# One 512-column matmul moves both activation halves in the feed-forward of layers 1 to 3

## The chip, the cores and the metric

The kernel runs on one core of a Trainium2 chip. The metric is device time in microseconds (us): the median of three runs. TensorE (PE in the profile) multiplies, VectorE (DVE) and ScalarE (ACT) work element by element, GpSimd (POOL) and SyncE (SP) mainly issue transfers.

## The reference

Four layers over 256 tokens of width 1024; each layer has a token mixer (forgetting attention, a state-space layer, a pooling mixer, forgetting attention again) and then a dense SwiGLU. Everything is float32.

```python
def swiglu(h, w_gate_up, w_down):
    g, u = jnp.split(h @ w_gate_up, 2, axis=-1)
    return (jax.nn.silu(g) * u) @ w_down

for i in range(DEPTH):                       # DEPTH = 4, D_MODEL = 1024, D_FF = 2816
    x = x + mixer_i(rms_norm(x, mix_norm_g[i]))
    x = x + swiglu(rms_norm(x, ffn_norm_g[i]), ffn_w_gate_up[i], ffn_w_down[i])
return rms_norm(x, final_norm_g)
```

## The kernel before, in words

Activations are kept transposed: 8 blocks of 128 features, 256 tokens (N) in the free dimension. Near-float32 precision comes from splitting every matmul operand into a high and a low half in the fp32r format: a weight unit arrives by DMA as `raw` (128 x 1024), ACT casts it to the high half (line 98), and DVE subtracts to make the low half (line 99); both halves stand in one tile `hl`. The activations `X` and the hidden layer `H` have halves too. `term` (line 158) multiplies one 128 x 128 weight piece with one activation block in three matmuls of 256 columns: weight-high by X-high, weight-low by X-high, weight-high by X-low. They add up in the same 256 columns of a PSUM bank. Each of the three loads its own weights.

The feed-forward of a layer (`ffn`, line 239) has a gate-up part and a down part. Gate-up makes 22 pairs of a gate tile G and an up tile U; each of the 44 tiles is one weight unit and 8 terms (24 matmuls). The first four tiles (two pairs) are computed block by block of X, alternating between four banks; after that the tiles go one after the other through the four `P` banks, so the G of one pair takes the bank that the G two pairs earlier left. `act` evicts a pair: `t` = G times the row scale R on DVE (line 248), silu on ACT (line 249), `h` = U times t on DVE (line 251), and the split of `h` into H-high (ACT, line 178) and H-low (DVE, line 179). Down makes 8 blocks of 22 terms into two `acc` banks, scales each by R (line 273), adds it to the residual x (line 237) and prepares what the next layer needs (`settled`, line 181).

Each engine runs its instructions in the order in which they stand in its queue; that order comes from a scheduler that rearranges the program's own order. Weights are fetched through 4 `raw` buffers and cast into 5 `hl` buffers, so a cast waits until PE is done with the unit that stood five places earlier. `rstd` (line 210) forms R between the stages: a matmul with ones over the squares (`sq`), a power on POOL, two transposes on PE and a copy on ACT.

Of the kernel before, what the change touches and what calls it, by code (L numbers as in the profile page):

```python
# [9 lines left out]
F32 = mybir.dt.float32  # L10
F32R = mybir.dt.float32r
AF = mybir.ActivationFunctionType
ALU = mybir.AluOpType
# [4 lines left out]
N = 256  # L18
DFF = 2816
NCH = DFF // 128  # L20
# [13 lines left out]
class Trunk:  # L34
# [128 lines left out]
    def dense(self, outs, X, ready=None):  # L163
        hls = [self.unit() for _ in outs]
        for k in range(8):
            for out, hl in zip(outs, hls):
                self.term(out, hl, slice(128 * k, 128 * k + 128), X, k, k == 0, k == 7)
                if k % 2 or len(outs) > 1 and (out is outs[1] or out is outs[-1]):
                    self.tick()

    def new_X(self, pool=None):
        return (pool or self.ap).tile([128, 2, 8, N], F32R, tag="X", name="X", bufs=1)

    def work(self, name="wk"):
        return self.ap.tile([128, N], F32, tag="wk", name=name, bufs=6)

    def split(self, hi, lo, src):
        self.nc.scalar.copy(hi, src)  # L178
# [2 lines left out]
    def settled(self, d, key):  # L181

        nc, x = self.nc, self.x[:, d]
        if d == 0:
            self.sq = self.ap.tile([128, N], F32, tag="sq", name="sq", bufs=2)
            if key is not None and key != 2:
                self.X = self.new_X()
        if key is not None and key != 2:
            g = self.gT[:, 8 * key + d:8 * key + d + 1]
            nc.scalar.activation(self.X[:, 0, d], x, AF.Identity, scale=g)  # L190
            nc.vector.scalar_tensor_tensor(out=self.X[:, 1, d], in0=x, scalar=g, in1=self.X[:, 0, d].bitcast(F32),
                                           op0=ALU.mult, op1=ALU.subtract)
        if key == 2:
            self.at(2, lambda: self.to_tokens(d))
        if d == 0:
            nc.scalar.activation(self.sq, x, AF.Square, scale=1.0 / 32.0)
        else:
            s = self.work("s")
            nc.scalar.activation(s, x, AF.Square, scale=1.0 / 32.0)  # L199
            nc.vector.tensor_tensor(out=self.sq, in0=self.sq, in1=s, op=ALU.add)  # L200
        if key is None:
            if d == 0:
                self.xg = self.ap.tile([128, 8, N], F32, tag="X", name="xg", bufs=1)
# [35 lines left out]
    def ffn(self, l):  # L239
        nc = self.nc  # L240
        X, key = self.X, l + 1 if l + 1 < self.layers else None
        with self.tc.tile_pool(name="hidden", bufs=1, reuse_waits="tile") as hp:
            H = hp.tile([128, 2, NCH, N], F32R, name="H")
            R = self.R

            def act(i, G, U):
                t = self.work("t")
                nc.vector.tensor_tensor(out=t, in0=G, in1=R, op=ALU.mult)  # L248
                nc.scalar.activation(t, t, AF.Silu)  # L249
                h = self.work("h")  # L250
# [3 lines left out]
            outs = [self.bank(t)[:, 0:N] for t in ("acc", "acc", "P", "P")]  # L254
            self.dense(outs, X)
            act(0, outs[0], outs[1])
            act(1, outs[2], outs[3])
            for i in range(2, NCH):
                G, U = self.bank("P")[:, 0:N], self.bank("P")[:, 0:N]
                self.dense([G], X)  # L260
                self.dense([U], X)
                act(i, G, U)
            for d in range(8):
                o = self.bank("acc")[:, 0:N]
                for u, ks in enumerate((8, 8, 6)):
                    hl = self.unit()
                    for k in range(ks):
                        f = 8 * u + k
                        self.term(o, hl, slice(128 * k, 128 * k + 128), H, f, f == 0, f == NCH - 1)
                        if k % 2:  # L270
                            self.tick()
                t = self.work("t")
                nc.vector.tensor_tensor(out=t, in0=o, in1=R, op=ALU.mult)
                self.add(d, t)
                self.settled(d, key)

    def fox(self, l, j):
        nc, a, X = self.nc, self.a, self.X
# [5 lines left out]
        cols = (slice(0, 352), slice(352, 704), slice(704, 1040))  # L284
        seg = [[banks[3 * t + s][:, 0:cols[s].stop - cols[s].start] for s in range(3)] for t in range(2)]
        for k in range(8):
            hl = self.unit()
            for t in range(2):
                tok = slice(t * 128, t * 128 + 128)
                for s, (xs, ws) in enumerate(((0, 0), (0, 1), (1, 0))):  # L290
                    for o, c in zip(seg[t], cols):
                        self.mm(o, X[:, xs, k, tok], hl[:, ws, c], k == 0 and s == 0, k == 7 and s == 2)
                self.tick()
        rs, R = self.rs, self.R
        self.lf, self.nd, self.c = [], [], []
# [80 lines left out]
    def heads(self, hp, q, kT, oT):  # L376
# [40 lines left out]
        self.split(oT[:, 0, hp], oT[:, 1, hp], op[:, 0:N])  # L417

    def to_tokens(self, d):
        nc = self.nc  # L420
# [14 lines left out]
    def poolmix(self, l):  # L435
# [7 lines left out]
        for d in range(8):  # L443
            o = self.bank("acc")[:, 0:N]
            f = slice(d * 128, d * 128 + 128)
            self.mm(o[:, 0:128], self.xt[:, 0, f], sb0[:, d // 2, 0:128], True, False)
            self.mm(o[:, 128:256], self.xt[:, 1, f], sb1[:, d // 2], False, False)
            self.mm(o[:, 128:144], self.xt[:, 0, f], sb0[:, d // 2, 128:144], False, True)
            g = self.gT[:, 8 * l + d:8 * l + d + 1]
            nc.scalar.activation(X[:, 0, d], o, AF.Identity, scale=g)  # L450
            nc.vector.scalar_tensor_tensor(out=X[:, 1, d], in0=o, scalar=g, in1=X[:, 0, d].bitcast(F32),
                                           op0=ALU.mult, op1=ALU.subtract)
        for u in range(2):
            hl = self.unit()
# [379 lines left out]
    def emit(self, m, u, CX, KT, sx, G):  # L834
# [11 lines left out]
        self.split(G[:, 0, m], G[:, 1, m], g)  # L846
        self.emitted = m + 1

    def final(self):
# [128 lines left out]
```

## Time and profile before

| | |
|---|---|
| runs | 1190.84, 1191.64, 1192.45 us; median 1191.64 |
| the profiled execution | 1194.52 us; its span, first to last instruction, 1192.7 us |
| mean granted TensorE clock | 0.98 |
| PE busy | 1145.8 us, 96% of the span |
| DVE busy | 823.4 us, 69% |
| ACT busy | 622.3 us, 52% |

A busy PE is one with at least one matmul in its pipeline; a matmul's own row lasts longer than the distance to the next one, since neighbours overlap. The distance from start to start is therefore what a matmul costs in a dense row of them, and it is read from the first start of a merged row, its count, and the start of what follows.

### The profile page before, as it was taken

Reading aid. Unit: us, or ns where it says so; the run is one execution under the profiler, and the core shown is the slowest. Engines: PE = TensorE matmul, PEld = TensorE weight load, DVE = VectorE, ACT = ScalarE, POOL = GpSimd, SP = SyncE. Lnnn points to the kernel's source line nnn. Section 1 sums busy time; section 2 is a strip of 40 time slices with the busy share of each in tenths; the row PEclk is TensorE's granted clock in tenths of the full one; section 3 lists DMA queues with packets and bytes.
Section 4 is the critical chain, followed back from the end, with each engine's and each line's share of the span. In section 5 each row is a group of like instructions: output and inputs, shape, how many; then the busy total and the mean of one; then the engine's idle time right before and its main releaser. Section 6 shows DMA issues by size and latency. Waiting matters only on the chain. (4 is left out here: it accounts for less than half of the span.)

```text
span 1192.7 us, 25313 instructions
## 1 busy us (share of the span) xinstructions
PE 1145.8 (96%) x10238; PEld 1115.4 (94%) x10238; DVE 823.4 (69%) x1525; ACT 622.3 (52%) x1094; POOL 160.6 (13%) x186
## 2 busy tenths in 40 slices
PE   6989999999999999999999899999998999999996
PEld 6878999999999889999999899999997899999996
DVE  6799987877659766666655576665656677666563
ACT  5546777677743144544444564444445566544441
POOL 1288001111102210000000000000006730000000
PEclk9889999999999899999999899999999999999998
DMA  7645466777879626566566355666665554765561
GB/s 270 183 158 152 156 211 234 248 241 223 284 254 334 240 75 194 190 182 186 177 179 186 104 175 180 188 176 182 191 189 184 151 160 120 221 190 179 177 185 44
DMA packets 63492, 225.16 MB, mean 189 GB/s; under 512 B 7824, under 2 KB 8192, under 8 KB 63248
## 3 DMA queue, kind: packets, MB, share of 16 engines
q1 hardware_dynamic: 56304, 200.83, 54.5%
q0 software_dynamic: 6208, 21.64, 5.7%
q8 instruction: 80, 1.31, 0.4%
q10 hardware_dynamic: 864, 1.09, 0.3%
q14 instruction: 36, 0.29, 0.1%
HBM read 208.81 MB, written 14.71 MB: 187 GB/s over the span
## 5 line engine op out<-in xcount | busy, mean ns | idle before, releaser
L156 PE MATMUL P<-X,hl 128*128 128x256 f32 x5520 | 685.5, 284 | 0.0
L156 PEld LDWEIGHTS P<-X,hl 128*128 128x128 f32 x5520 | 668.3, 190 | 8.0 <-issue 7.5
L99 DVE TENSOR_TENSOR hl<-raw,hl 128x1024 fp32r<-128x1024 f32 (+3 forms) x363 | 438.3, 1208 | 209.0 <-ACT hl L98 205.7
L98 ACT CAST hl<-raw 128x1024 fp32r<-128x1024 f32 (+3 forms) x363 | 371.8, 1026 | 389.8 <-issue 174.9
L156 PE MATMUL acc<-H,hl 128*128 128x256 f32 x2112 | 253.6, 281 | 0.7 <-DVE H L179 0.7
L156 PEld LDWEIGHTS acc<-H,hl 128*128 128x128 f32 x2112 | 250.6, 188 | 1.5 <-DVE H L179 0.9
L156 PE MATMUL acc<-X,hl 128*128 128x256 f32 x480 | 71.1, 292 | 5.4 <-DVE X L179 3.6
L221 POOL TENSOR_TENSOR rs<-rs,mhalf 128x2 f32<-128x2 f32 x9 | 6.5, 724 | 486.4 <-DVE rs L220 486.4
L156 PEld LDWEIGHTS acc<-X,hl 128*128 128x128 f32 x480 | 62.4, 193 | 8.4 <-DVE X L179 4.4
L372 POOL TENSOR_SCALAR nb<-nb,c 128x128 f32<-128x128 f32 (+1 forms) x64 | 64.1, 1015 | 1.1
L251 DVE TENSOR_TENSOR h<-P,t 128x256 f32<-128x256 f32 x84 | 35.5, 422 | 30.6 <-PE P L156 30.6
L393 ACT ACTIVATE pt<-pt,st 128x128 f32<-128x128 f32 (+1 forms) x64 | 28.5, 446 | 30.0 <-DVE st L391 30.0
L248 DVE TENSOR_TENSOR t<-P,R 128x256 f32<-128x256 f32 x84 | 35.5, 422 | 10.6 <-PE P L156 8.0
L249 ACT ACTIVATE t<-t 128x256 f32<-128x256 f32 x88 | 36.5, 414 | 11.9 <-DVE t L248 11.7
L178 ACT CAST H<-h 128x256 fp32r<-128x256 f32 x88 | 35.3, 402 | 12.3 <-DVE h L251 12.3
L156 PE MATMUL P<-hl,X 128*128 128x336 f32 (+1 forms) x192 | 40.0, 330 | 0.0
L179 DVE TENSOR_TENSOR H<-h,H 128x256 fp32r<-128x256 f32 x88 | 36.9, 419 | 0.2 <-ACT H L178 0.2
L156 PE MATMUL acc<-hl,X 128*128 128x352 f32 x96 | 25.0, 343 | 10.2 <-ACT X L190 6.6
L190 ACT ACTIVATE X<-x,gT 128x256 fp32r<-128x256 f32 x56 | 28.3, 505 | 11.8 <-DVE x L237 7.6
L156 PEld LDWEIGHTS P<-hl,X 128*128 128x128 f32 x192 | 33.4, 197 | 0.0
L199 ACT ACTIVATE s<-x 128x256 f32<-128x256 f32 x63 | 25.6, 406 | 12.4 <-DVE x L237 12.4
L406 PE MATMUL tp<-cst,pt 128*128 128x128 f32 x96 | 18.2, 302 | 11.8 <-DVE pt L397 10.5
(165 smaller groups left out, 800.7 us busy)
## 6 DMA issues: line engine op xcount, KB each, us to landing
raw<-in_w_gu SPq DMA_DIRECT2D x176, 512.0 KB, 3.9
raw<-in_w_dn SPq DMA_DIRECT2D x64, 512.0 KB, 3.6
raw<-in_w_qk SPq DMA_DIRECT2D x32, 512.0 KB, 3.7
raw<-in_w_dn SPq DMA_DIRECT2D x32, 384.0 KB, 3.4
raw<-in_w_fo SPq DMA_DIRECT2D x16, 512.0 KB, 3.7
raw<-in_w_glu SPq DMA_DIRECT2D x16, 512.0 KB, 4.8
raw<-in_w_vf SPq DMA_DIRECT2D x15, 520.0 KB, 3.7
nb<-nd POOLq DMA_DIRECT2D x24, 256.0 KB, 5.8
```

The lines of the kernel that those rows point to most:

```text
L98: nc.scalar.copy(hl[:, 0, s], raw[:, s])
L99: nc.vector.tensor_tensor(out=hl[:, 1, s], in0=raw[:, s], in1=hl[:, 0, s].bitcast(F32), op=ALU.subtract)
L156: self.nc.tensor.matmul(out, lhsT=lhsT, rhs=rhs, start=start, stop=stop)
L178: self.nc.scalar.copy(hi, src)
L179: self.nc.vector.tensor_tensor(out=lo, in0=src, in1=hi.bitcast(F32), op=ALU.subtract)
L190: nc.scalar.activation(self.X[:, 0, d], x, AF.Identity, scale=g)
L199: nc.scalar.activation(s, x, AF.Square, scale=1.0 / 32.0)
L248: nc.vector.tensor_tensor(out=t, in0=G, in1=R, op=ALU.mult)
L249: nc.scalar.activation(t, t, AF.Silu)
L251: nc.vector.tensor_tensor(out=h, in0=U, in1=t, op=ALU.mult)
L372: nc.gpsimd.tensor_scalar(out=nb[:, i], in0=nb[:, i], scalar1=self.c[t][:, 4 * n + i:4 * n + i + 1], scalar2=None, op0=ALU.add)
L393: nc.scalar.activation(pt, pt, AF.Exp, bias=st[:, 0:1], scale=-1.0, accum_out=st[:, 1:2])
```

## The change

In the feed-forward of layers 1, 2 and 3 a term is two matmuls in place of three. The two halves of an activation block now lie next to each other (`[128, 8, 2, N]` in place of `[128, 2, 8, N]`, and the same for H), so that the high half of the weights moves both halves as 512 columns into a whole bank: columns 0 to 255 get weight-high by X-high, columns 256 to 511 get weight-high by X-low. The low half of the weights then moves X-high into columns 256 to 511. `fold` adds the two sums when the bank is evicted: ACT copies the second half of the bank to SBUF (`lo`), DVE adds it to the first half, and what was read from the bank before (the multiplication by R, or U times t) now reads that sum. Layer 0 and all mixers keep the three matmuls; only the indices of X and H change there. The work tiles have 8 buffers in place of 6, and `xg` has memory of its own.

```diff
     def term(self, out, hl, cols, X, k, start, stop):
-        self.mm(out, hl[:, 0, cols], X[:, 0, k], start, False)
-        self.mm(out, hl[:, 1, cols], X[:, 0, k], False, False)
-        self.mm(out, hl[:, 0, cols], X[:, 1, k], False, stop)
+        self.mm(out, hl[:, 0, cols], X[:, k, 0], start, False)
+        self.mm(out, hl[:, 1, cols], X[:, k, 0], False, False)
+        self.mm(out, hl[:, 0, cols], X[:, k, 1], False, stop)
...
+    def wide(self, o, hl, s, X, k, first, last):
+        self.mm(o, hl[:, 0, s], X[:, k].rearrange("p a n -> p (a n)"), first, False)
+        self.mm(o[:, N:], hl[:, 1, s], X[:, k, 0], False, last)
+
+    def fold(self, o):
+        nc = self.nc
+        lo, t = self.work("lo"), self.work("t")
+        nc.scalar.copy(lo, o[:, N:])
+        nc.vector.tensor_tensor(out=t, in0=o[:, 0:N], in1=lo, op=ALU.add)
+        return t
...
-            H = hp.tile([128, 2, NCH, N], F32R, name="H")
+            H = hp.tile([128, NCH, 2, N], F32R, name="H")
...
+            wide = l > 0
+            cut = (lambda z: z) if wide else (lambda z: z[:, 0:N])
...
             def act(i, G, U):
-                t = self.work("t")
-                nc.vector.tensor_tensor(out=t, in0=G, in1=R, op=ALU.mult)
+                t = self.fold(G) if wide else self.work("t")
+                nc.vector.tensor_tensor(out=t, in0=t if wide else G, in1=R, op=ALU.mult)
                 nc.scalar.activation(t, t, AF.Silu)
-                h = self.work("h")
-                nc.vector.tensor_tensor(out=h, in0=U, in1=t, op=ALU.mult)
-                self.split(H[:, 0, i], H[:, 1, i], h)
+                h = self.fold(U) if wide else self.work("h")
+                nc.vector.tensor_tensor(out=h, in0=h if wide else U, in1=t, op=ALU.mult)
+                self.split(H[:, i, 0], H[:, i, 1], h)
...
-                o = self.bank("acc")[:, 0:N]
+                o = cut(self.bank("acc"))
...
-                        self.term(o, hl, slice(128 * k, 128 * k + 128), H, f, f == 0, f == NCH - 1)
+                        s = slice(128 * k, 128 * k + 128)
+                        (self.wide if wide else self.narrow)(o, hl, s, H, f, f == 0, f == NCH - 1)
...
-                t = self.work("t")
-                nc.vector.tensor_tensor(out=t, in0=o, in1=R, op=ALU.mult)
+                t = self.fold(o) if wide else self.work("t")
+                nc.vector.tensor_tensor(out=t, in0=t if wide else o, in1=R, op=ALU.mult)
                 self.add(d, t)
```

On all engines the order is the same, instruction by instruction, until the first matmul of layer 1's feed-forward, and SP and POOL keep their order to the end. PE has 1584 matmuls fewer. Three places show how the rest moved.

PE where layer 1's feed-forward begins, before (acc_6107, acc_6108, P_6109 and P_6110 are the banks of the first four tiles, tp_6146 and tp_6160 belong to `rstd`):

```order
L156 MATMUL acc_6107<-X_5664,hl_6026 128x256 x3
L156 MATMUL acc_6108<-X_5664,hl_6055 128x256 x2
L156 MATMUL tp_6146<-cst_73,sq_5663 128x1 x2
L156 MATMUL acc_6108<-X_5664,hl_6055 128x256
L156 MATMUL P_6109<-X_5664,hl_6113 128x256 x3
L226 MATMUL tp_6160<-cst_73,rs_6092 128x128 x2
L156 MATMUL P_6110<-X_5664,hl_6118 128x256 x3
```

The same place now (tp_6141 and tp_6152 are the two of `rstd`):

```order
L156 MATMUL acc_6107<-X_5664,hl_6026 128x512
L156 MATMUL acc_6107<-X_5664,hl_6026 128x256
L156 MATMUL acc_6108<-X_5664,hl_6055 128x512
L156 MATMUL acc_6108<-X_5664,hl_6055 128x256
L156 MATMUL tp_6141<-cst_73,sq_5663 128x1 x2
L156 MATMUL P_6109<-X_5664,hl_6113 128x512
L156 MATMUL P_6109<-X_5664,hl_6113 128x256
L156 MATMUL P_6110<-X_5664,hl_6118 128x512
L244 MATMUL tp_6152<-cst_73,rs_6092 128x128 x2
L156 MATMUL P_6110<-X_5664,hl_6118 128x256
```

Each three of 256 columns became one of 512 and one of 256; the two steps of `rstd` stand at nearly the same place.

DVE from there on, before (hl_6128 is the low half for the sixth tile; P_6109 the third tile's bank, which the seventh tile takes over):

```order
L248 TENSOR_TENSOR t_6236<-acc_6107,R_6093 128x256
L99 TENSOR_TENSOR hl_6128<-raw_6121,hl_6128 128x1024
L251 TENSOR_TENSOR h_6239<-acc_6108,t_6236 128x256
L248 TENSOR_TENSOR t_6243<-P_6109,R_6093 128x256
L99 TENSOR_TENSOR hl_6254<-raw_6126,hl_6254 128x1024
L179 TENSOR_TENSOR H_6106<-h_6239,H_6106 128x256
L251 TENSOR_TENSOR h_6246<-P_6110,t_6243 128x256
```

And now:

```order
L99 TENSOR_TENSOR hl_6128<-raw_6121,hl_6128 128x1024
L186 TENSOR_TENSOR t_6205<-acc_6107,lo_6204 128x256
L99 TENSOR_TENSOR hl_6234<-raw_6126,hl_6234 128x1024
L269 TENSOR_TENSOR t_6205<-t_6205,R_6093 128x256
L186 TENSOR_TENSOR t_6211<-acc_6108,lo_6210 128x256
L99 TENSOR_TENSOR hl_6255<-raw_6232,hl_6255 128x1024
L99 TENSOR_TENSOR hl_6291<-raw_6253,hl_6291 128x1024
L272 TENSOR_TENSOR t_6211<-t_6211,t_6205 128x256
L186 TENSOR_TENSOR t_6218<-P_6109,lo_6217 128x256
```

The instruction that empties P_6109 stood behind three others, one of them a weight split; now it stands behind eight, four of them weight splits. Layer 3's feed-forward begins in the same order.

DVE at the end of layer 3, before (acc_14363 is the last block's bank):

```order
L200 TENSOR_TENSOR sq_13825<-sq_13825,s_14359 128x256
L273 TENSOR_TENSOR t_14433<-acc_14363,R_12252 128x256
L237 TENSOR_TENSOR x_72<-t_14433,x_72 128x256
L200 TENSOR_TENSOR sq_13825<-sq_13825,s_14436 128x256
L220 TENSOR_SCALAR rs_14441<-tp_14443 128x2
```

And now (lo_13314 is ACT's copy of the bank's second half):

```order
L218 TENSOR_TENSOR sq_12842<-sq_12842,s_13262 128x256
L186 TENSOR_TENSOR t_13315<-acc_13266,lo_13314 128x256
L295 TENSOR_TENSOR t_13315<-t_13315,R_11508 128x256
L255 TENSOR_TENSOR x_72<-t_13315,x_72 128x256
L218 TENSOR_TENSOR sq_12842<-sq_12842,s_13320 128x256
L238 TENSOR_SCALAR rs_13325<-tp_13327 128x2
```

One DVE addition, with a copy on ACT ahead of it, came between the last matmul and the rest.

## Rows read from the trace of the kernel before

**Rows 1.** The page: busy time by engine, and the granted clock in 40 slices.

```profile
PE 1145.8 (96%) x10238; PEld 1115.4 (94%) x10238; DVE 823.4 (69%) x1525; ACT 622.3 (52%) x1094; POOL 160.6 (13%) x186
PEclk9889999999999899999999899999999999999998
```

**Rows 2.** Busy time by stretch: layer 2's gate-up.

```profile
core 0: us, PE busy (x) PEld busy (x) DVE busy (x) ACT busy (x) POOL busy (x), PEclk, DMA share, GB/s
692.50:807.30 114.80, 114.80 (x966) 114.80 (x966) 76.77 (x107) 57.32 (x86) 0.00 (x0) 1.00 0.63 191
```

**Rows 3.** Timeline of PE, layer 2: start, duration, instructions merged (x their number).

```profile
692.45 115.16 PE L156 MATMUL P<-X,hl 128*128 128x256 f32 x966
807.45 62.51 PE L156 MATMUL acc<-H,hl 128*128 128x256 f32 x528
869.80 0.32 PE L156 MATMUL acc<-hl,X 128*128 128x352 f32 x1
```

**Rows 4.** Timeline of PE in layer 3's attention projection, 352 and 336 columns.

```profile
882.99 0.48 PE L156 MATMUL acc<-hl,X 128*128 128x352 f32 x2
883.31 1.74 PE L156 MATMUL P<-hl,X 128*128 128x336 f32 x10
884.89 0.48 PE L156 MATMUL acc<-hl,X 128*128 128x352 f32 x2
```

**Rows 5.** Groups by form, DVE and ACT, gate-up of layer 2: busy us, mean ns.

```profile
L99 DVE TENSOR_TENSOR hl<-raw,hl 128x1024 fp32r<-128x1024 f32 x42 | 51.3, 1224 | 24.5 <-ACT hl L98 24.5
L248 DVE TENSOR_TENSOR t<-P,R 128x256 f32<-128x256 f32 x21 | 8.9, 424 | 4.0 <-PE P L156 3.1
L179 DVE TENSOR_TENSOR H<-h,H 128x256 fp32r<-128x256 f32 x21 | 8.8, 419 | 0.2 <-ACT H L178 0.2
L98 ACT CAST hl<-raw 128x1024 fp32r<-128x1024 f32 x41 | 42.9, 1049 | 54.9 <-issue 51.1 <-PE P L156 2.3 <-DMA raw<-in_w_gu 1.4
L249 ACT ACTIVATE t<-t 128x256 f32<-128x256 f32 x22 | 9.1, 413 | 0.0
L178 ACT CAST H<-h 128x256 fp32r<-128x256 f32 x21 | 8.4, 401 | 0.0
L227 ACT COPY R<-tp 128x256 f32<-128x256 f32 x1 | 0.4, 373 | 0.1
```

**Rows 6.** Timeline of all engines where layer 1's first four tiles end.

```profile
474.02 0.43 PE L226 MATMUL tp<-cst,rs 128*128 128x128 f32 x2 [0.47 <-POOL rs L221]
...
480.90 1.05 ACT L98 CAST hl<-raw 128x1024 fp32r<-128x1024 f32 x1 [6.04 <-PE acc L156]
481.01 115.17 PE L156 MATMUL P<-X,hl 128*128 128x256 f32 x966
481.98 1.23 DVE L99 TENSOR_TENSOR hl<-raw,hl 128x1024 fp32r<-128x1024 f32 x1 [0.63 <-ACT hl L98]
```

**Rows 7.** Timeline where layer 2's and layer 3's feed-forward begin.

```profile
685.97 0.48 DVE L191 SCALAR_TENSOR_TENSOR X<-x,gT,X 128x256 fp32r<-128x256 f32 x1 [0.58 <-ACT X L190]
687.73 0.49 DVE L191 SCALAR_TENSOR_TENSOR X<-x,gT,X 128x256 fp32r<-128x256 f32 x1 [0.58 <-ACT X L190]
...
1002.30 0.43 PE L226 MATMUL tp<-cst,rs 128*128 128x128 f32 x2
```

**Rows 8.** Timeline at the ends of layers 1, 2 and 3.

```profile
660.18 0.42 DVE L273 TENSOR_TENSOR t<-acc,R 128x256 f32<-128x256 f32 x1
...
872.69 0.42 DVE L200 TENSOR_TENSOR sq<-sq,s 128x256 f32<-128x256 f32 x1
874.24 0.50 PE L156 MATMUL tp<-cst,sq 128*128 128x1 f32 x4
...
1181.79 0.42 DVE L273 TENSOR_TENSOR t<-acc,R 128x256 f32<-128x256 f32 x1 [6.00 <-PE acc L156]
1182.25 0.42 DVE L237 TENSOR_TENSOR x<-t,x 128x256 f32<-128x256 f32 x1
```

**Rows 9.** Busy time by stretch after layer 1's end (columns as in Rows 2).

```profile
664.50:671.30 6.80, 6.80 (x31) 6.49 (x32) 2.25 (x5) 1.95 (x5) 0.00 (x0) 0.50 0.13 53
```

More of the change, by code (lines that the diff above doesn't have):

```diff
@@ L158, in term, with dense @@
     def term(self, out, hl, cols, X, k, start, stop):
-        self.mm(out, hl[:, 0, cols], X[:, 0, k], start, False)
-        self.mm(out, hl[:, 1, cols], X[:, 0, k], False, False)
-        self.mm(out, hl[:, 0, cols], X[:, 1, k], False, stop)
-    def dense(self, outs, X, ready=None):
+        self.mm(out, hl[:, 0, cols], X[:, k, 0], start, False)
+        self.mm(out, hl[:, 1, cols], X[:, k, 0], False, False)
+        self.mm(out, hl[:, 0, cols], X[:, k, 1], False, stop)
+    def dense(self, outs, X, wide=False):
         hls = [self.unit() for _ in outs]
@@ L166, in dense, with narrow @@
             for out, hl in zip(outs, hls):
-                self.term(out, hl, slice(128 * k, 128 * k + 128), X, k, k == 0, k == 7)
+                s = slice(128 * k, 128 * k + 128)
+                if wide:
+                    self.wide(out, hl, s, X, k, k == 0, k == 7)
+                else:
+                    self.term(out, hl, s, X, k, k == 0, k == 7)
                 if k % 2 or len(outs) > 1 and (out is outs[1] or out is outs[-1]):
                     self.tick()
+    def narrow(self, o, hl, s, X, k, first, last):
+        self.term(o, hl, s, X, k, first, last)
+    def wide(self, o, hl, s, X, k, first, last):
[7 more added lines that the diff above has]
+        return t
     def new_X(self, pool=None):
-        return (pool or self.ap).tile([128, 2, 8, N], F32R, tag="X", name="X", bufs=1)
+        return (pool or self.ap).tile([128, 8, 2, N], F32R, tag="X", name="X", bufs=1)
     def work(self, name="wk"):
-        return self.ap.tile([128, N], F32, tag="wk", name=name, bufs=6)
+        return self.ap.tile([128, N], F32, tag="wk", name=name, bufs=8)
     def split(self, hi, lo, src):
@@ L202, in settled @@
             if d == 0:
-                self.xg = self.ap.tile([128, 8, N], F32, tag="X", name="xg", bufs=1)
+                self.xg = self.ap.tile([128, 8, N], F32, tag="xg", name="xg", bufs=1)
             if d % 2:
@@ L258, in ffn @@
             for i in range(2, NCH):
-                G, U = self.bank("P")[:, 0:N], self.bank("P")[:, 0:N]
-                self.dense([G], X)
-                self.dense([U], X)
+                G, U = cut(self.bank("P")), cut(self.bank("P"))
+                self.dense([G], X, wide)
+                self.dense([U], X, wide)
                 act(i, G, U)
             for d in range(8):
-                o = self.bank("acc")[:, 0:N]
+                o = cut(self.bank("acc"))
                 for u, ks in enumerate((8, 8, 6)):
@@ L291, in fox @@
                     for o, c in zip(seg[t], cols):
-                        self.mm(o, X[:, xs, k, tok], hl[:, ws, c], k == 0 and s == 0, k == 7 and s == 2)
+                        self.mm(o, X[:, k, xs, tok], hl[:, ws, c], k == 0 and s == 0, k == 7 and s == 2)
                 self.tick()
@@ L416, in heads @@
                             pT[t][:, e, s * 128:s * 128 + 128], s == 0, s == t)
-        self.split(oT[:, 0, hp], oT[:, 1, hp], op[:, 0:N])
+        self.split(oT[:, hp, 0], oT[:, hp, 1], op[:, 0:N])
     def to_tokens(self, d):
@@ L845, in emit @@
         nc.scalar.activation(g.rearrange("p (j r) -> p r j", r=4), yv, AF.Gelu_apprx_tanh)
-        self.split(G[:, 0, m], G[:, 1, m], g)
+        self.split(G[:, m, 0], G[:, m, 1], g)
         self.emitted = m + 1
```

13 lines of the change are left out of this document (7 added, 6 removed).

## The prediction

> **What bounds the kernel now.** The page comes first: PE is busy for 96% of the span and its granted clock is near full in nearly every slice, DVE 69%, ACT 52% [rows 1]. Next the stretch of a gate-up part: 114.80 us in which PE has no idle time at clock 1.00 while DVE works 76.77 and ACT 57.32 [rows 2]. The timeline of PE then shows one unbroken row of 966 matmuls, and 528 more in the down part [rows 3]. So in the feed-forward nothing but the distance between matmul starts counts: (807.45 - 692.45) / 966 = 119.05 ns in gate-up, (869.80 - 807.45) / 528 = 118.09 ns in down. At the granted clock of 2.4 GHz 256 columns stream in 106.67 ns, so 12.4 and 11.4 ns a matmul are surplus. What the change is worth is a question about this surplus, because the columns stay: 3 x 256 before, 512 + 256 after.
>
> **What a 512-column matmul costs.** No row shows one. The nearest are the attention projection's: 12 matmuls of 352, 352 and 336 columns (346.7 on average) from 882.99 to 884.89, 158.3 ns each [rows 4], where 346.7 columns stream in 144.4 ns. The surplus is 13.9 ns there, against 12.4 at 256: it grows little with the columns. Three readings follow.
> - Surplus per instruction, as at 256: 213.33 + 12.4 = 225.7 ns.
> - A line through both points (39.3 ns for 90.7 columns, 0.433 ns a column): 158.3 + 165.3 x 0.433 = 229.9 ns.
> - The bounds: a column cannot go faster than the granted clock, so at best 213.3; at worst all of the surplus is paid per column, and 512 cost twice 256, 238.1 (236.2 in down).
>
> I take 228, between the first two: what the 346.7 columns leave over, carried to 512 (213.3 + 13.9 = 227.2), lies there too.
>
> **What is saved.** A term before is 3 x 119.05 = 357.2 ns, after 228 + 119.05 = 347.1: 10.1 ns less in gate-up. In down 354.3 - 346.1 = 8.2. There are 3 x 44 x 8 = 1056 terms in gate-up and 3 x 176 = 528 in down. Not all save: of the 32 terms of a layer's first four tiles, those bring nothing that stand ahead of a wait for another engine, since PE only reaches that wait earlier. In layer 2 new blocks of X arrive 1.76 us apart [rows 7] and the 12 matmuls on a block take 12 x 119 = 1.43 us, so all 32 hide; in layer 1 some 13 terms precede the transposes that wait for POOL at 474.02 [rows 6], in layer 3 some 28 those at 1002.30 [rows 7]. That leaves 1056 - 73 = 983. Sum: 983 x 10.1 + 528 x 8.2 = 9.9 + 4.3 = 14.2 us.
>
> **What is added in the middle of a layer.** Each tile gets one copy on ACT (0.37, as R from PSUM) and one addition on DVE (0.42, as line 248). DVE per pair before: 2 x 1.22 + 3 x 0.42 = 3.7 us, now 4.55; ACT 2 x 1.05 + 0.41 + 0.40 = 2.9, now 3.65 [rows 5]. A pair now takes PE 16 x 347 ns = 5.55 us, so both still fit (82% and 66%), and I cost the folds inside a layer, 51 of a layer's 52, at nothing but the start below. The cover is the buffers: a weight split may start when the unit five places earlier is done, four units or 11 us ahead of its use, and a bank is wanted again three units, 8.3 us, after its last matmul. The copy waits for PE, and behind it on ACT stands the next weight cast, which waits for the same matmul anyway. Without that cover PE would wait out whatever the two are late: 0.1 us in each of the 60 pairs that follow a layer's first two would be 6 us.
>
> **What is added where a layer starts.** The first four tiles end together, and their four folds meet the weight splits for the next units. The seventh tile needs the third one's bank, and DVE empties it ninth in the new order of layer 1: four splits of 1.22 and five short ones of 0.42 make 7.0 us. Before, PE passes from the fourth tile to the fifth at 481.01 + 6 x 0.119 = 481.72, and DVE's first split begins at 481.98, 0.26 later, fed by the cast that waited for the first tile [rows 6]. So the bank comes free 7.3 us, with the handing over to PE 7.4 us, after the fifth tile's start; PE wants it after two tiles, 5.55 us. A stall of 1.85 us that the trace of before does not have, since three instructions stood ahead there. Bounds: 0 if DVE begins earlier, 3.0 if ACT's table load before the silu also lies on the way. Layer 3 has the same order, so 3.7 us for both. In layer 2, R comes later but the table is loaded and one split fewer stands ahead: I count nothing. The tile after that finds its bank some 0.2 us early, so nothing follows.
>
> **What is added where a layer ends.** The last block's eviction (660.18 in layer 1, 1181.79 in layer 3) starts a chain for which PE waits [rows 8]; ahead of it come now the copy and the addition, 0.37 + 0.42 + 0.05 for handing over (1182.25 less 1181.79 + 0.42 is 0.04) = 0.85 us, twice: 1.7 us. At layer 2's end PE goes on with the attention projection; the squares are ready at 872.69 + 0.42 = 873.11 and PE asks at 874.24 [rows 8], so 1.1 us of cover hold the 0.85; without it, 0.85 more. The longer idle at layer 1's end stands just before a stretch at clock 0.50 that lasts 6.8 us [rows 9]; if its length or place moves, up to half of it, 3.4 us, goes either way. I count nothing and keep it for the range.
>
> **The sum.** 14.2 - 3.7 - 1.7 = 8.8 us less. Against the profiled execution's 1194.52 that is 1185.7; that execution is 2.9 us above the median of the runs, so the same 8.8 from 1191.64 give 1182.8 us.
>
> **Rivals.**
> 1. *The surplus is paid per column.* Then the wide matmul costs 238.1, nothing is saved, and the 5.4 us of stalls and tails remain: 1191.64 + 5.4 = 1197.0, slower. Saving and cost balance where 512 columns cost 233.8 ns ((983 x 238.1 + 528 x 236.2 - 5400) / 1511); above that the kernel is slower. For it: the surplus at 346.7 columns is larger than at 256. Against: pure proportion would make 161.2 of 346.7 columns, measured 158.3. The Trainium skill's page "TensorE: Matmul & The Clock Gate", section "Back-to-back issue gap", speaks for it: it gives a warm gap of N / 2.4 + 2.5 ns, so only 2.5 ns hang on an instruction, and one instruction less in 1511 terms would bring 3.8 us, less than the 5.4; the time by that rule would be 1193.2. The trace does not agree with the rule as it stands: 256 columns would take 109.2 by it, and the row shows 119.05.
> 2. *The surplus comes with a weight load that does not quite fit under 256 columns.* Under 512 it fits, the wide matmul costs 213.3, and 36.4 us are saved: less 5.4, 1160.6. Against: 346.7 columns leave 38 ns more room for the load than 256 and still show 13.9 ns. With half of the surplus gone (219.5), 1170.
> 3. *ACT and DVE wait for each other in each pair,* since the copy is on one and the addition on the other. With no overlap at all 3.65 + 4.55 = 8.2 us a pair against 5.55, 2.65 x 60 pairs: over 1300 us. Against: the same sum before, 6.6, is above the 5.71 that a pair took, and PE never waited [rows 2, 5]. A tenth of it would already undo the gain and give 1199.
>
> **How the numbers follow.** The forecast, 512 columns between 222 and 232 ns: 0.60, with 1174 to 1189, and the clock's 3.4 us on either side. Rival 1, above 232: 0.20, 1189 to 1197. Rival 2, under 222: 0.12, 1161 to 1175. Rival 3: 0.08, 1195 and more. The range 1170 to 1196 leaves out about half of rival 2 and of rival 3 and the worst of rival 1. What a measurement can tell from no change is 0.2%, 2.4 us: under 1189.3 faster, over 1194.0 slower. Faster: 0.59 + 0.12 + 0.03 of rival 1 = 0.74; same: 0.01 + 0.09 = 0.10; slower: 0.08 of rival 1 and 0.08 of rival 3 = 0.16.
>
> **What would show it right or wrong.** A term in the dense part of gate-up should take 347 ns from start to start, and the matmul after one of 512 columns should start 228 ns behind it; 233.8 or more there makes the whole wrong. PE should wait once, 1.9 us, for DVE's addition (the new line 186) at the seventh tile of layers 1 and 3 and at no other tile; a wait at many tiles is rival 3. The eviction chains of layers 1 and 3 should be 0.85 us longer, and up to 469 us the two traces should agree.

## The result and the profile after

The changed kernel takes 1181.73 us (median of four runs, 1180.33 to 1183.60), the kernel before 1191.36 in the same session (1190.84 to 1192.45): ratio 0.9919, 95% interval 0.9902 to 0.9936. Forecast were 1182.8 us. The profiled execution took 1182.6 us, its span 1180.8 us; before it was 1194.52 and 1192.7.

The page of the changed kernel, busy time and granted clock, against [rows 1]:

```profile
PE 1130.3 (96%) x8654; PEld 1032.4 (87%) x8654; DVE 885.1 (75%) x1681; ACT 675.7 (57%) x1250; POOL 160.6 (14%) x186
PEclk9889999999999999999999899999999999999998
```

There are 1584 matmuls fewer, one for each term of layers 1 to 3, and DVE and ACT carry the 156 folds. The timeline of PE in layer 2 (start, duration, instructions merged; the rows x644 and x352 hold matmuls of 512 and of 256 columns in turn), against [rows 3]:

```profile
687.78 111.86 PE L156 MATMUL P<-X,hl 128*128 128x512 f32 x644
799.49 61.17 PE L156 MATMUL acc<-H,hl 128*128 128x512 f32 x352
860.50 0.33 PE L156 MATMUL acc<-hl,X 128*128 128x352 f32 x1
```

PE is still one unbroken row. A term is two starts, before it was three: 2 x (799.49 - 687.78) / 644 = 346.9 ns in gate-up, before 357.2; 2 x (860.50 - 799.49) / 352 = 346.6 in down, before 354.3. Taken apart by the single starts, the wide matmul takes 229.9 ns and the narrow one after it 117.0. DVE still fits, as the same stretch by engine shows, against [rows 2]:

```profile
687.60:799.40 111.80, 111.80 (x646) 98.57 (x646) 93.55 (x150) 72.37 (x130) 0.00 (x0) 1.00 0.63 196
```

New waits of PE are few: the seventh tile of layer 1 (of layer 3 likewise at 1002.37), the first tiles of layer 2, and the chains at the ends of layers 1 and 3, against [rows 6, 8]:

```profile
677.64 1.31 PE L156 MATMUL P<-X,hl 128*128 128x512 f32 x6 [1.27 <-ACT y L483]
...
483.90 105.70 PE L156 MATMUL P<-X,hl 128*128 128x512 f32 x608 [1.01 <-DVE t L186]
...
655.41 0.41 PE L445 MATMUL tp<-cst,x 128*128 128x128 f32 x2 [1.93 <-DVE x L255]
...
1171.86 0.61 PE L156 MATMUL tp<-cst,sq 128*128 128x1 f32 x4 [2.80 <-DVE sq L218]
```

Before comparing the two traces stage by stage, what differs from one execution to the next has to be set aside. Up to layer 1's feed-forward the instructions are the same in number and order, yet the changed kernel gets there 4.2 us earlier (464.54 against 468.74). These are stretches at half the clock (0.50, 1.2 GHz) between 400 and 433 us before, and then after the change the one at that place and the one behind layer 1's end:

```profile
408.50:418.70 10.20, 9.88 (x141) 9.07 (x144) 5.05 (x9) 0.56 (x1) 2.35 (x2) 0.50 0.27 97
429.00:432.40 3.40, 3.40 (x57) 3.28 (x61) 0.71 (x1) 0.00 (x0) 0.43 (x1) 0.50 0.00 0
```

```profile
408.10:414.90 6.80, 6.80 (x85) 6.16 (x88) 3.16 (x7) 0.00 (x0) 0.00 (x0) 0.50 0.28 90
657.30:667.50 10.20, 9.18 (x43) 8.83 (x44) 3.44 (x8) 2.83 (x6) 0.68 (x1) 0.50 0.15 51
```

Half the clock for 13.6 us in place of 6.8 costs some 3.4 us ahead of layer 1's feed-forward. Another 1.0 us lies in layer 0's down part, where PE in the trace of before waits 0.73 us for the low half of H (at 290.77) and in the trace of after doesn't; of the other kernels that keep this layer as it is, some wait there and some don't. After layer 1's end the clock goes the other way (10.2 against 6.8 us in [rows 9]), and in layer 3's attention the half clock lasts 3.4 us after and 6.8 before. How long these stretches are differs from one execution to the next, also in work that the change doesn't touch, so the first row of the table is not the change's. The difference of the two spans, 11.9 us, by stages (us, after less before; feed-forward from its first matmul):

| stage | layer 1 | layer 2 | layer 3 |
|---|---|---|---|
| ahead of the feed-forward, with clock and waits | -4.20 | +1.56 | +0.40 |
| gate-up, with its stall | -2.38 | -2.99 | -2.45 |
| down | +0.06 | -1.34 | -1.34 |
| from the last matmul to the end | | | +0.77 |

The feed-forward and the two longer ends (0.73 in layer 1, within its +1.56, and 0.77 in layer 3) make -8.9 us; forecast were -8.8.

### The profile page after: what moved, and what is told of

Its sections match the earlier page's. It is cut to its first block, busy times and chain, and to the rows that moved or that the text cites. A ratio compares the mean times of both kernels' runs of the same rounds, so it can differ in the third digit from the quotient of the medians.

```text
span 1180.8 us, 22351 instructions
## 1 busy us (share of the span) xinstructions
PE 1130.3 (96%) x8654; PEld 1032.4 (87%) x8654; DVE 885.1 (75%) x1681; ACT 675.7 (57%) x1250; POOL 160.6 (14%) x186
## 5 line engine op out<-in xcount | busy, mean ns | idle before, releaser
L156 PE MATMUL P<-X,hl 128*128 128x256 f32 (+1 forms) x4512 | 676.2, 309 | 3.3 <-DVE t L186 2.0
L156 PEld LDWEIGHTS P<-X,hl 128*128 128x128 f32 x4512 | 615.1, 190 | 53.1 <-issue 7.5
L156 PE MATMUL acc<-H,hl 128*128 128x256 f32 (+1 forms) x1584 | 250.3, 319 | 0.0
L156 PEld LDWEIGHTS acc<-H,hl 128*128 128x128 f32 x1584 | 224.2, 188 | 22.7 <-issue 0.6
L185 ACT COPY lo<-P 128x256 f32<-128x256 f32 x126 | 46.7, 372 | 108.5 <-PE P L156 108.5
L186 DVE TENSOR_TENSOR t<-P,lo 128x256 f32<-128x256 f32 x126 | 53.2, 424 | 44.4 <-ACT lo L185 44.3
L156 PE MATMUL acc<-X,hl 128*128 128x256 f32 (+1 forms) x432 | 68.3, 300 | 5.4 <-DVE X L197 3.6
L156 PEld LDWEIGHTS acc<-X,hl 128*128 128x128 f32 x432 | 56.7, 189 | 9.9 <-DVE X L197 4.2
L270 ACT ACTIVATE t<-t 128x256 f32<-128x256 f32 x88 | 36.8, 419 | 15.0 <-DVE t L269 11.9
L209 DVE SCALAR_TENSOR_TENSOR X<-x,gT,X 128x256 fp32r<-128x256 f32 x56 | 26.8, 480 | 3.7 <-ACT X L208 3.7
L272 DVE TENSOR_TENSOR t<-t 128x256 f32<-128x256 f32 x66 | 28.0, 424 | 1.9
```

The costliest lines, as they stand in the source:

```text
L185: nc.scalar.copy(lo, o[:, N:])
L186: nc.vector.tensor_tensor(out=t, in0=o[:, 0:N], in1=lo, op=ALU.add)
L209: nc.vector.scalar_tensor_tensor(out=self.X[:, d, 1], in0=x, scalar=g, in1=self.X[:, d, 0].bitcast(F32), op0=ALU.mult, op1=ALU.subtract)
L272: nc.vector.tensor_tensor(out=h, in0=h if wide else U, in1=t, op=ALU.mult)
```

## The experiments

All kernels are the changed kernel with the edit shown, where nothing else is said; ratios are against the kernel before, run beside them. "Place" means where the high half of a weight tile begins, counted in bytes from where the moving X or H begins, modulo 256; the low half lies 64 bytes further in all of them.

**The parts of the change.** First the new layout of X, H and the work tiles with the old three matmuls, and the wide matmul cut in two.

```diff
 e1_layout
-            wide = l > 0
+            wide = False
 e2_split
-        self.mm(o, hl[:, 0, s], X[:, k].rearrange("p a n -> p (a n)"), first, False)
+        self.mm(o[:, 0:N], hl[:, 0, s], X[:, k, 0], first, False)
+        self.mm(o[:, N:], hl[:, 0, s], X[:, k, 1], False, False)
```

> The new layout of X and H, but three matmuls of 256 columns everywhere and no fold. Theory (the saving comes from one instruction less in each term): gate-up stays at 119.05 ns a matmul and down at 118.1, no stall at the seventh tile, 1191.4 us like the kernel before, within 2.4. Rival (the saving comes from where X and H lie now, since the 256-column matmuls of the changed kernel take 117.0 ns and not 119.05): 117.0 ns a matmul, 351 a term, some 8 us less than before, 1183.

> The changed kernel with its 512-column matmul cut into two of 256 columns with the same weights, into the same two halves of the bank; fold and eviction stay. Theory (one instruction less): a term is back at 357 ns, and the stalls and tails of the folds stay, 1191.4 + 3.8 = 1195 us. Rival (the place of X and H): 351 ns a term, 1187 to 1188 us.

The layout alone is worth nothing: 1190.58 us, ratio 0.9988 (0.9970 to 1.0006), and 3 x (802.85 - 689.74) / 950 = 357.2 ns a term, as before. PE in layer 2 of that kernel:

```profile
689.74 113.28 PE L156 MATMUL P<-X,hl 128*128 128x256 f32 x950
802.85 62.51 PE L156 MATMUL acc<-H,hl 128*128 128x256 f32 x528
```

The cut variant surprises: 1188.75 us, 0.9973 (0.9954 to 0.9992), though it has three matmuls a term again and keeps folds, stalls and ends. Its gate-up term is 3 x (807.83 - 695.28) / 966 = 349.5 ns:

```profile
695.28 112.71 PE L156 MATMUL P<-X,hl 128*128 128x256 f32 x966
807.83 62.48 PE L156 MATMUL acc<-H,hl 128*128 128x256 f32 x528
```

So of the 10.3 ns that the change takes off a gate-up term, 7.7 come without one instruction less, and only 2.6 with it; in down, where the cut term is 354.1, it is 0.2 and 7.5. A fixed surplus for each instruction would give the same in both.

**The added waits.** The narrow form for the first four tiles and the last down block of layers 1 to 3; and, apart from it, no fold at all.

```diff
 e3_ends
-            outs = [cut(self.bank(t)) for t in ("acc", "acc", "P", "P")]
-            self.dense(outs, X, wide)
+            outs = [self.bank(t)[:, 0:N] for t in ("acc", "acc", "P", "P")]
+            self.dense(outs, X)
...
             for d in range(8):
+                if d == 7:
+                    wide, cut = False, lambda z: z[:, 0:N]
 e4_nofold
     evictions read o[:, 0:N] directly; no copy, no addition
```

> The changed kernel, but the first four tiles and the last down block of layers 1 to 3 go with three matmuls and without a fold. Theory (the stall at the seventh tile comes from four folds among weight splits, the longer tail from the last fold): PE no longer waits 1.2 us there in layers 1 and 3, the ends are 0.75 us shorter twice, 66 terms of down cost 7 to 10 ns more each (0.6 us), 1178.7 us, 3 less than the changed kernel. Rival (the wait has another cause, or another wait takes its place): 1181.7 us or more.

> The changed kernel without the fold: the second half of each bank is not added, so weight-low and X-low do not reach the result. Theory (in the middle of a layer the folds cost nothing): as much faster as the stalls and tails were long, 2 x 1.2 + 2 x 0.75 = 3.9 us, 1177.8 us, terms still 347 ns. Rival (the copies and additions also slow the dense part, by reading PSUM while PE writes there): terms under 347 ns and 1176 us or less.

Narrow ends: 1178.07 us, 0.9882 (0.9855 to 0.9909). The wait at the seventh tile is gone, and the wait at layer 1's end is back from 1.93 to 1.21 us, as in the kernel before:

```profile
483.61 106.65 PE L156 MATMUL P<-X,hl 128*128 128x512 f32 x614
...
659.60 0.41 PE L447 MATMUL tp<-cst,x 128*128 128x128 f32 x2 [1.21 <-DVE x L255]
```

No fold: 1177.18 us, 0.9875 (0.9853 to 0.9897), and the term of gate-up stays 2 x (589.28 - 477.59) / 644 = 346.9 ns:

```profile
477.59 111.85 PE L156 MATMUL P<-X,hl 128*128 128x512 f32 x644
589.28 9.26 PE L156 MATMUL acc<-H,hl 128*128 128x512 f32 x52
```

The folds inside a layer cost nothing, then. By the medians those at its ends cost some 3.7 to 4.6 us, which narrow ends give back; the kernels ran in different sessions, and the intervals are 2 to 3 us wide on either side. The waits in the trace of the changed kernel come to 3.8 us (below).

**Order.** What does the cut variant gain by? Only the order of the three is changed here, all into the same 256 columns.

```diff
 e8_order (no second half, no fold)
+        self.mm(o, hl[:, 0, s], X[:, k, 0], first, False)
+        self.mm(o, hl[:, 0, s], X[:, k, 1], False, False)
+        self.mm(o, hl[:, 1, s], X[:, k, 0], False, last)
```

> Three 256-column matmuls per term in layers 1 to 3, all into the same 256 columns, no second half and no addition at eviction, as in the kernel before; only their order is new: high weights on X-high, high weights on X-low, low weights on X-high (before: the low weights stood second). It tells what made the split variant's term 349.6 ns in gate-up (before 357.2) though it has as many matmuls as before. Theory A (two neighbours that load the same weights): 349.6 ns per term in gate-up and about 354 in down, whole time 1186 to 1190 us. Theory B (two neighbours that add into different halves of the bank): 357.2 ns and 354.2, whole time 1190 to 1192.

1183.33 us, 0.9935 (0.9906 to 0.9963): two lines swapped bring, by the medians, most of what the whole change brings. Gate-up 3 x (797.90 - 689.81) / 928 = 349.4 ns a term, down 354.0:

```profile
689.81 108.25 PE L156 MATMUL P<-X,hl 128*128 128x256 f32 x928
797.90 62.48 PE L156 MATMUL acc<-H,hl 128*128 128x256 f32 x528
860.21 0.32 PE L156 MATMUL acc<-hl,X 128*128 128x352 f32 x1
```

**Place.** Sorted by the five buffers of `hl`, the terms fall into two groups, and the buffers' addresses agree: they begin 8320 bytes apart, so in gate-up a weight tile lies at place 0 or 128, in down of layers 2 and 3 at 64 or 192. Before, gate-up took 353.3 ns at 0 and 359.7 at 128; with the new order 353.8 and 346.6; with the wide matmul 347.1 and 346.7. The order gains at one of the two places only. Three sweeps move weights, X and H, for the wide matmul, the new order and the old one.

```diff
 e7_sweep (e10_sweepn on e8_order, e14_sweepo on e1_layout)
-        hl = self.wp.tile([128, 2, 1040], F32R, tag="hl", name="hl", bufs=HL_BUFS)
+        o = (8 * (h % 8) - 48) % 64
+        hl = self.wp.tile([128, 2176], F32R, tag="hl", name="hl", bufs=HL_BUFS)
+        hl = hl[:, o:o + 2080].rearrange("p (a n) -> p a n", a=2)
```

> The changed kernel with other places in the SBUF, nothing else: the high half of weight tile n starts at byte 32*(n mod 8) of a 256-byte row (low half 64 bytes further), and the moving tiles start at byte 192, 0 and 64 (X of layers 1, 2, 3) and 96, 64 and 128 (H of layers 1, 2, 3) of one. Theory A (the length of a term depends on where the weights and the moving activation lie against each other): within one layer the eight places of the weights give terms that differ by 5 to 10 ns, repeating every 8 tiles; with H at 128 (layer 3) weights at 64 give 340.4 ns and weights at 192 give 350 ns, as those two places did in the changed kernel; layer 1's down part, whose H lay at 224 and took 354 ns, falls below 350 for some weights. Theory B (the differences go by the buffer in the rotation or by the position in a block, not by the address): terms stay 346.9 ns in gate-up and 346.6 on average in down, whatever the byte. The whole time is 1180 to 1184 us in B, 1176 to 1188 in A.

> The order variant (three matmuls of 256 columns per term, the two on the high weights as neighbours, no second half) with the weights' places swept as in the sweep before, H of layer 1 at byte 128. It gives for the three narrow matmuls the table that the wide ones have. Theory A (a term's length is set by place against place for narrow ones too, and the fused matmul saves only one instruction): at the best place the narrow term is 343 to 347 ns, 2 to 5 ns over the wide one's best 341.7; at 0 and at 128 bytes it repeats 353.8 and 346.7. Theory B (a narrow matmul has a fixed surplus of 7 to 12 ns that the wide one halves): no place brings the narrow term under 350 ns, apart from the 346.7 already seen at 128. Whole time 1180 to 1186 us.

> The layout variant (three matmuls of 256 columns per term in the order of the kernel before, no second half) with the same sweep of places. Averaged over the eight places the wide term took 347.9 ns and the narrow one with the high weights as neighbours 354.0 in gate-up. Theory A (the order of the three has a worth of its own): the old order averages 356 to 358 ns over the places. Theory B (order only shifts at which place a term is long; what the order variant gained was the luck of its two places): the old order averages 353 to 355 ns, with its good and bad places elsewhere than those of the new order. In both, 353.3 at place 0 is the layout variant's value; at 128 it was 359.7 there. Whole time 1185 to 1192 us.

Single runs: 1181.36, 1187.53 and 1184.66 us. Mean length of a term in gate-up by place, from the starts of its matmuls (in each layer the last 32 tiles, four tiles of 8 terms for every place; the three layers, whose X begin at bytes 192, 0 and 64, agree within 0.2 ns):

| place | 0 | 32 | 64 | 96 | 128 | 160 | 192 | 224 | mean |
|---|---|---|---|---|---|---|---|---|---|
| wide | 346.9 | 346.7 | 352.5 | 352.9 | 347.0 | 346.6 | 341.7 | 349.2 | 347.9 |
| new order | 354.6 | 353.1 | 354.8 | 355.4 | 350.6 | 357.3 | 353.0 | 352.8 | 354.0 |
| old order | 352.8 | 354.5 | 353.5 | 349.2 | 350.5 | 359.2 | 352.9 | 354.8 | 353.4 |

The length goes by place, and that holds from layer to layer. It is not the place alone: at 128 the old order took 359.7 ns in the kernel before and 350.5 here, among other neighbours. Averaged over places, in this one sequence of neighbours, the order is worth nothing (354.0 against 353.4), and the wide matmul 5.5 ns a term (in down of layers 2 and 3 of the same kernels the wide term averages 348.3, the old order 354.7). The kernel before stood, with 357.2, 3.8 ns above the old order's mean. So theory B of the last sweep holds. Theory A of the sweep before it (343 to 347 ns for the new order at its best place) does not: no place in the two narrow sweeps is under 349.2.

In layer 1's down part H begins at byte 224, so the weights lie at places 96 and 224. In seven of its eight blocks two transposes for the next mixer interrupt the row, here for the first time:

```profile
589.43 9.84 PE L156 MATMUL acc<-H,hl 128*128 128x512 f32 x55
599.13 0.44 PE L445 MATMUL tp<-cst,x 128*128 128x128 f32 x2
599.33 0.94 PE L156 MATMUL acc<-H,hl 128*128 128x256 f32 x4
```

Without the interrupted terms a wide term takes 351.0 ns there (352.0 at 96, 350.3 at 224), near what the table has for these places, against 353.9 in the kernel before. An interruption lengthens the terms that it falls on by 0.30 us, in the kernel before by 0.22.

**Can the best place be had everywhere?** All weights at place 192; then the same with narrow ends and every eighth tile at 160; then also layer 0; and the narrow order with all at 128.

```diff
 e9_align, on the changed kernel: weights at byte 192, X and H at byte 0 of a 256-byte row
 e11_kick, on e3_ends
+        o = 56 if any(s <= h < s + 68 and (h - s) % 8 == 4 for s in (124, 194, 294)) else 0
 e12_kick0, on e11_kick (layer 0's weights and X moved in the same way)
-            wide = l > 0
+            wide = True
 e13_order128, on e8_order: weights at byte 192, X and H at byte 64
```

> The changed kernel with every weight tile's high half at byte 192 of a 256-byte row and X and H of layers 1 to 3 at byte 0, so that in all their terms the weights lie 192 bytes (that is, 64 bytes short of a row) past the moving activation; the weight tiles keep their order and size of data. Theory A (place against place sets the term): 341.7 ns per term in gate-up of all three layers (from 346.9) and 341 to 345 in down (from 354.3 in layer 1, 346.6 in layers 2 and 3); some 1008 terms of gate-up by 5.2 ns, 352 of down by 2 to 6 and 176 of layer 1's down by 9 to 13: 7.5 to 10 us off, 1172 to 1175 us. Theory B (the table of the sweep came from neighbours in the rotation, not from the place): 346.9 stays, 1181 to 1183 us. The weights of the other stages change place as well (all at 192), which may move the time before layer 1 by a microsecond or two either way.

> The variant with narrow ends (first four tiles and last down block of layers 1 to 3 as before) with every weight tile at byte 192 of a row and X and H of layers 1 to 3 at byte 0, except every eighth weight tile, which lies at byte 160: in the aligned run all terms of a layer took either 340 ns or 350 ns, changing only where TensorE paused, and in the sweep every tile at 192 that followed one at 160 took 340. Theory A (the place of one tile decides into which of the two rhythms the next ones fall): at most 8 terms of 349 per 64, the others 340, so 341 to 342 ns in gate-up of all three layers and 341 to 345 in down; 960 terms of gate-up by 5.2 ns, 308 of down by 2 to 5, 154 of layer 1's down by 9 to 13: 7 to 8.5 us under the narrow-ends variant's 1178.1, so 1169.5 to 1171. Theory B (which rhythm it is, is chance, or set by what else happens in a layer): some layers at 350 throughout as in the aligned run, 1174 to 1180 us and runs that spread by over 8 us.

> The variant before, with layer 0's feed-forward done in the same way (fused matmul, narrow ends, the same places). Layer 0's terms are 359 to 361 ns in gate-up and 357 to 360 in down. Theory A (the place and the rhythm set the term, in every layer alike): 342 ns there too, 320 terms of gate-up by 18 ns and 154 of down by 15: 8 us under the variant before, 1161 to 1164 us. Theory B (layer 0's terms are longer because its VectorE and ScalarE carry the tables' preparation beside the evictions, and the fold makes them late): waits of the P tiles for VectorE in layer 0, and under 4 us gained, 1166 us or more.

> The order variant (three 256-column matmuls, the two on the high weights as neighbours; no second half, no addition) with all weights 128 bytes past X and H in layers 1 to 3, where its gate-up terms took 346.7 ns. It asks how much of the change's gain the kernel before could have had without the fused matmul. Theory A (order and place are the larger part): 346.7 to 350.6 ns per term in gate-up and 350 in down, from 349.6 and 354 (layer 1: 363): some 1 to 3 us by gate-up, 1.4 by down of layers 2 and 3 and 2 by layer 1, so 1177 to 1181 us, level with the changed kernel. Theory B (that place was good only among tiles at place 0): 353 ns per term, 1183 to 1187 us.

Aligned: 1177.36 us, 0.9862 (0.9811 to 0.9913), but the four runs lie between 1170.62 and 1183.71. Its profiled execution is the slowest of the four and shows what may lie behind that. Layer 2, then layer 3:

```profile
690.70 112.86 PE L158 MATMUL P<-X,hl 128*128 128x512 f32 x644
803.39 61.76 PE L158 MATMUL acc<-H,hl 128*128 128x512 f32 x352
...
1007.00 103.61 PE L158 MATMUL P<-X,hl 128*128 128x512 f32 x608 [1.15 <-DVE t L188]
1110.44 60.00 PE L158 MATMUL acc<-H,hl 128*128 128x512 f32 x352
```

Neither expectation of that run came true (341.7 everywhere, or 346.9): the same instructions on the same places take 2 x 112.69 / 644 = 350.0 ns a term in layer 2 and 2 x 103.44 / 608 = 340.3 in layer 3. Single terms, start to start (ns), show that they don't scatter; they keep a rhythm until something breaks it:

```
aligned, layer 2          350 350 350 350 350 350 350 350
aligned, layer 3          340 340 340 340 340 340 340 340
aligned, layer 1: the 7th tile's wait, then   422 350 350 350   (340 ahead of it)
changed kernel, layer 1   346 347 346 347 346 348 346 347
changed kernel, layer 1's down   353 353 354 353 353 354  and  344 349 353 344 349 354
```

In the steady ones a few terms add up to a multiple of 10 ns: 340, 350, 3 x 346.7 = 1040, 3 x 353.3 = 1060; of the last one it takes nine, 3140. The place sets which rhythms occur, and where two occur, what PE last came through seems to choose: in layer 1 the rhythm changed right behind the wait at the seventh tile, but in layer 3 the same wait left it at 340. With layers 1 and 2 at 340 as well, some 830 terms by 10 ns, an estimated 8 us of the 13 between the runs would go; that the fast executions had this is not shown, as none of them was profiled.

The tile at 160 was meant to throw every layer into the 340 rhythm. It did the opposite: from its second occurrence on all of gate-up between two such tiles took 350 ns in layers 1 to 3, and the time is 1181.18 us, 0.9910 (0.9882 to 0.9937), no better than narrow ends alone. Theory A of that run is wrong; its theory B had the 350 and the spread, but chance it is not, since the three layers repeat it. With layer 0 as well it is 1178.72, 0.9893 (0.9870 to 0.9916), 2.5 us less by the medians, within the intervals. Layer 0's undisturbed terms in gate-up did fall as theory A said, from 353.6 to 342.3 ns (the 359 to 361 of the expectation were not free of what the tables' matmuls between them cost), but waits took it all, as theory B had it: in the profiled executions layer 0's feed-forward takes 203.6 us, in the variant before 201.9. The first wait is at a P tile, the second at the down part's last block of H, where the variant before waits 0.75 us:

```profile
271.76 1.66 PE L158 MATMUL P<-X,hl 128*128 128x512 f32 x8 [1.14 <-DVE t L188]
...
289.81 10.40 PE L158 MATMUL acc<-H,hl 128*128 128x512 f32 x50 [3.29 <-DVE H L202]
```

The narrow order at place 128: 1188.28 us, 0.9962 (0.9936 to 0.9988), no better than at its old places, and the runs spread widest of all (1177.68 to 1194.52). Layer 1, then layer 2:

```profile
476.74 116.08 PE L158 MATMUL P<-X,hl 128*128 128x256 f32 x966
592.66 7.60 PE L158 MATMUL acc<-H,hl 128*128 128x256 f32 x62
...
689.80 111.11 PE L158 MATMUL P<-X,hl 128*128 128x256 f32 x951
800.75 61.76 PE L158 MATMUL acc<-H,hl 128*128 128x256 f32 x528
```

3 x 115.92 / 966 = 360.0 and 3 x 110.95 / 951 = 350.0 ns: two rhythms again. Neither theory of that run had 360.

Of the versions that compute everything, the one with narrow ends (1178.07, runs from 1174.66 to 1182.49) and that with layer 0 (1178.72, 1174.32 to 1182.27) are lowest but for the aligned one; both beat the kernel before, and narrow ends lie 0.4% under the changed kernel by the ratios (0.9882 against 0.9919, measured in different sessions; the intervals overlap a little). The aligned kernel reached 1170.62 once, but not reliably.

## Why the prediction was right

- **The bound** was named rightly: PE's start-to-start distance. No copy, addition or transfer inside a layer became the limit, and taking the folds away left the term at 346.9.
- **The length of the wide matmul.** 228 ns were taken between 213.3 and 238.1; measured are 229.9, and the term is 346.9 for 347.1. The line through the 256-column row and the mixed rows of 346.7 columns on average [rows 3, 4] gave 229.9 and was the better guess than the mean. But the reason was not what the text said, and that the number came out is in good part luck. The 12.4 ns are no property of an instruction: the same three matmuls take from 349.2 to 359.2 ns a term by place. The rows that the estimate came from were measured at places of this program, and the changed kernel kept those places. Of the 10.3 ns saved in a gate-up term, the sweeps put 3.8 down to the old order standing badly (357.2 against its mean of 353.4), 5.5 to one instruction less (353.4 against 347.9), and 1.0 to the wide order standing well (346.9). At 5.5 ns the saving would be 5.5 x 1511 = 8.3 us in place of 14.2, and the gain 2.9 us with the forecast's 5.4 of waits, 4.5 with the 3.8 measured (2 x 1.17 + 0.73 + 0.77).
- **Down** was mis-sized: 8.2 ns for 528 terms, 4.3 us; measured 2.7 in layers 2 and 3 together, 7.6 ns for 352 terms, and nothing in layer 1. All three layers were costed by layer 2's row. In layer 1, where H lies elsewhere, a term saves only 2.9 ns (353.9 to 351.0), 0.5 us for 176 terms, and the seven interruptions cost 0.08 us more each, which takes that back. With the weights at place 192 (aligned run) the undisturbed terms there average 342.2, and the down part falls from 63.76 to 62.57 us.
- **The seventh tile's wait**: place, cause and number right, the size 1.17 us for 1.85. DVE's queue there, as forecast four splits and five short ones:

```profile
477.45 1.23 DVE L99 TENSOR_TENSOR hl<-raw,hl 128x1024 fp32r<-128x1024 f32 x1 [6.85 <-ACT hl L98]
478.60 0.42 DVE L186 TENSOR_TENSOR t<-acc,lo 128x256 f32<-128x256 f32 x1
478.93 1.22 DVE L99 TENSOR_TENSOR hl<-raw,hl 128x1024 fp32r<-128x1024 f32 x1
480.06 0.42 DVE L269 TENSOR_TENSOR t<-t,R 128x256 f32<-128x256 f32 x1
480.40 0.42 DVE L186 TENSOR_TENSOR t<-acc,lo 128x256 f32<-128x256 f32 x1
480.73 2.35 DVE L99 TENSOR_TENSOR hl<-raw,hl 128x1024 fp32r<-128x1024 f32 x2
483.00 0.42 DVE L272 TENSOR_TENSOR t<-t 128x256 f32<-128x256 f32 x1
483.33 0.42 DVE L186 TENSOR_TENSOR t<-P,lo 128x256 f32<-128x256 f32 x1
```

  They run from 477.45 to 483.75, 6.30 us for 7.0: in this dense queue the next row begins 0.08 to 0.09 us before the last one ends (478.60 against 477.45 + 1.23), so summed durations are too long. The two errors, 1.7 us too much in down and 1.4 too much for the waits, cancel by chance.
- **Layer 2's start** was costed at nothing, and PE waits 1.27 us at 677.64, because the P bank still holds the pooling's result until ACT has read it; the forecast sign "and at no other tile" fails here. The wait hides, as forecast of that layer's first tiles: X's blocks set the pace, and the dense row begins only 0.30 us later, counted from the feed-forward's first matmul (687.78 - 673.42 against 692.45 - 678.39).
- **The ends**: 0.85 forecast, 0.73 and 0.77 measured; narrow ends take both away (PE waits 1.21 and 1.94 us, as long as before or less). At layer 2's end the cover held: PE shows no wait for the squares. That the two traces agree up to 469 us was forecast too and did not come, for the clock and layer 0's wait.
- **Rival 1** (all of the surplus per column) is refuted: 229.9 is below its 232, and below the 233.8 at which nothing is gained. The rule that the Trainium skill's page "TensorE: Matmul & The Clock Gate" gives in its section "Back-to-back issue gap", a warm gap of N / 2.4 + 2.5 ns, which it calls that of an isolated matmul, would put one instruction less at 2.5 ns. Between the cut variant and the change it is 2.6 in gate-up, but 7.5 in down, and between the new order and the wide matmul 6.1 over eight places (354.0 less 347.9); the measurement decides, and the rule has no term for the place.
- **Rival 2** (213.3 ns) did not come. In the 340 rhythm the wide matmul takes 226 to 227 ns, so even there 13 ns stay. **Rival 3** did not come in layers 1 to 3; layer 0, where the tables are prepared beside it, shows what it would look like.

Not settled: why the place sets the rhythm. Weight loads run beside the matmuls all the time (114.80 us of each in 114.80 [rows 2]), and that their reads meet those of the activations would fit, but no run took the one without the other, so this is not shown. Which rhythm an interruption leaves behind was not predictable either.

## What to carry to other kernels

When PE is one dense row, measure the distance per weight buffer before reading a surplus as the price of an instruction; a mean over buffers mixes different lengths, and an edit that reorders matmuls or moves a tile can change it as much as one that removes an instruction. Judge such an edit over several places or with the place held, as one kernel at one place may be lucky. And where a new step is added at every eviction, keep it off the first tiles and the last block of a stage, where PE waits for exactly that chain.

## What the runs showed of the hardware

- 256-column matmuls in fp32r with the same instructions take 116.4 to 119.7 ns each on average in a sweep of the distance between weights and moving data modulo 256 bytes (349.2 to 359.2 a term), and the wide term 341.7 to 352.9.
- It is the distance that counts, not the byte of the moving operand alone: with H at byte 96, no multiple of 64, the undisturbed wide terms of the sweep average 348.7 ns in down, with H at 64 or 128 they average 348.3.
- The steady rows looked at keep rhythms whose sums are multiples of 10 ns (340, 350, 1040, 1060), and the same code on the same places can run at 340 or 350 ns a term (wide, layers 3 and 2 of the aligned run), 350 or 360 (narrow, layers 2 and 1 at place 128), for a whole gate-up part.
- Two transposes put between the terms of a dense row cost 0.30 us with wide terms (0.35 in the aligned run) and 0.22 us with narrow ones (layer 1's down part, seven times each).
